# Where the weights' high and low parts are kept in a two-layer hybrid encoder, and in which order the first ones are made

## Chip, cores, metric

The kernel runs on one core of one Trainium2 chip. The metric is the device time of one execution in microseconds. The median of three runs of the kernel before is 1534.49 us (1534.33 to 1534.7).

## What is computed

Two layers over 256 tokens of width 1024, in float32. Each layer has a mixer (one wide projection, three kinds of attention, gates, output projections) and a mixture of experts, each behind an RMS norm whose scale and shift come from a conditioning vector:

```python
for l in range(DEPTH):                       # DEPTH = 2
    mod = c_act @ ada_w[l] + ada_b[l]
    shift_m, scale_m, gate_m, shift_f, scale_f, gate_f = split(mod, 6)
    h = rms_norm(x, mix_norm_g[l]) * (1 + scale_m) + shift_m
    z = h @ w_in[l]                          # 1024 x 7680: q, k, v of three mixers, 3 gates
    o_a, o_n, o_d = diff_attention(z), neighbourhood_attention(z), dilated_attention(z)
    merged = g_a * (o_a @ w_proj_a) + g_n * (o_n @ w_proj_n) + g_d * (o_d @ w_proj_d)
    x = x + gate_m * (merged @ w_out[l])
    h = rms_norm(x, ffn_norm_g[l]) * (1 + scale_f) + shift_f
    x = x + gate_f * hier_moe(h)             # 32 experts, top 2 of one of 4 groups
out = rms_norm(x, final_norm_g)
```

## The kernel before

**Products in two parts.** The projections (`z`, the three `w_proj`, `w_out`) are done with float32 operands cut in two: a high part that ACT makes by a copy to the type `float32r`, and a low part, the rest, that VectorE makes by a subtraction. A product is then three matmuls, high with high, high with low, low with high (`gemm`, L333). For the normalised input these parts are `hi` and `lo` (`modulated`, L277), for the weights `whi` and `wlo` (`split`, L322). `split` takes a piece of 128 x 1024 numbers: two slices of 128 rows of the contraction by 512 columns. Its two results lie in tiles with the tags `w4a` and `w4b`, each with two buffers, so two pieces can be held at a time; a buffer comes free when the matmuls that read it are done.

**Chunks.** `w_in` is worked through in 15 chunks of 512 columns (`chunk`, L442, with `SEGS`, L41): 0 to 8 are queries, keys and values, 9 to 14 the gates. A chunk loads its 2 MB of weights (`load`, L385, two half pairs, see below), takes some loads of the conditioning weights for later use (`FILL`, L200; `ada_part`, L155, each with products of 128x512 on VectorE at L175 and some on ACT at L173), and calls `gemm` over four pieces. One piece gives 24 matmuls of 256 columns, or the same in 512 columns. The results are moved out of PSUM when the next chunk reaches its third piece (`HOLD`, `flush`): a rotary segment (`place`, L476) costs four ACT copies (L484), two VectorE products (L485, L486) and one GpSimd addition (L487).

**The first pieces.** In chunk 0 the first two pieces are split ahead of `modulated` (L429), with `early=True`: the copies on ACT are kept in program order, and the subtraction runs on GpSimd. `modulated` then takes the reciprocal root of the mean square (`rsqrt`, ten small VectorE instructions), spreads it over the partitions by two matmuls, and for each of 8 slices scales (VectorE, L292), adds the shift (ACT, L294, giving `hi`), and takes the rest (VectorE, L289, giving `lo`). The last of the four transposed blocks of the input is copied from PSUM on VectorE (L272) just before.

**Memory.** `slots` holds ten pairs of 128 x 4096 numbers; `slot` (L77) hands out halves. In the mixer eleven halves are taken as long-lived tiles at its start (L396): three for the gates (`G`, of which the third also holds the rotary tables), two each for queries, keys and values, two for work (`T0`, `T1`); with the transposed input that is six pairs. The other four pairs carry the streams of `w_in` and of the conditioning weights. A one-element write by GpSimd (L398) makes each long tile taken early.

**Order.** The tile framework plans the order on each engine: among instructions that are ready in its own model of time, the one that is earlier in the program goes first, and a tile is given its place at its first write. `keep_in_program_order` pins one instruction behind the one traced before it on the same engine. On the chip every engine works its list in that order. The attention of a layer is spread among the chunks by the plan; so are the loads, all issued by SP.

**After the mixer** `moe` (L694) streams the experts' weights, 2 MB a load, through the same ten pairs.

Of the kernel before, what the change touches and what calls it, by code (L numbers as in the profile page):

```python
# [60 lines left out]
class Kernel:  # L61
# [197 lines left out]
    def raw_t(self, c):  # L259

        nc = self.nc
        p = self.acc()
        for kk in range(2):
            k = 2 * c + kk
            for t in range(2):
                nc.tensor.transpose(p[:, kk * 256 + t * P:kk * 256 + (t + 1) * P],
                                    self.x[:, t, k * P:(k + 1) * P], self.ident)
        to, p = self.xT[:, 2 * c:2 * c + 2, :], p.rearrange("p (k n) -> p k n", k=2)
        if c < 3:
            nc.scalar.copy(to, p)  # L270
        else:
            self.rest = lambda: self.tc.keep_in_program_order(nc.vector.tensor_copy(to, p))  # L272

    def hilo(self):
        return (self.wk.tile([P, KD, 256], F32R, name=nm, tag=tag) for nm, tag in (("hi", "w8a"), ("lo", "w8b")))

    def modulated(self, l):  # L277

# [9 lines left out]
        def low(k):  # L288
            nc.vector.scalar_tensor_tensor(lo[:, k, :], xT[:, k, :], shift[:, k:k + 1], hi[:, k, :].bitcast(F32),  # L289
                                           op0=OP.add, op1=OP.subtract)  # L290
        for k in range(KD):
            i = nc.vector.scalar_tensor_tensor(xT[:, k, :], xT[:, k, :], scale[:, k:k + 1], R,  # L292
                                               op0=OP.mult, op1=OP.mult)
            nc.scalar.activation(hi[:, k, :], xT[:, k, :], AF.Identity, bias=shift[:, k:k + 1])  # L294
            if k > 1:
                self.tc.keep_in_program_order(i)
            if k:
                low(k - 1)
        low(KD - 1)
        return hi, lo  # L300

# [19 lines left out]

    def split(self, w, early=False):  # L322

        nc, n = self.nc, w.shape[1]
        whi, wlo = (self.wk.tile([P, n, 1024 // n], F32R, name=f"{nm}{n}", tag=tag, bufs=2)
                    for nm, tag in (("whi", "w4a"), ("wlo", "w4b")))
        c = nc.scalar.copy(whi, w)  # L327
        if early:
            self.tc.keep_in_program_order(c)
        (nc.gpsimd if early else nc.vector).tensor_sub(wlo, w, whi.bitcast(F32))  # L330
        return whi, wlo
# [46 lines left out]
    def mixer(self, l, fill):  # L378
# [16 lines left out]
        M = self.xT.rearrange("p k n -> p (k n)")  # L395
        tiles = [self.slot("long") for _ in range(11)]  # L396
        for b in tiles:
            nc.gpsimd.memset(b[:, 2047:2048], 0.0)  # L398
        G, (Q0, Q1, K0, K1, V0, V1, T0, T1) = tiles[:3], tiles[3:]
        ga = [G[i // 4][:, 512 * (i % 4):512 * (i % 4 + 1)] for i in range(12)]  # L400
        tok = [M[:, t * D:(t + 1) * D] for t in range(2)]
# [6 lines left out]
        self.dmask = [K1[:, 1536:], V0[:, 1536:]]  # L408
        self.rope = G[2][:, 1536:].rearrange("p (c n) -> p c n", c=2)
        self.subg = T0[:, 1664:1792]  # L410
# [10 lines left out]
        if l == 0:  # L421
            self.new_sums()
            for t in range(2):
                for half in range(2):
                    hs = slice(half * 512, (half + 1) * 512)
                    self.square(t, half, self.x[:, t, hs], G[t][:, hs])
            for c in range(4):
                self.raw_t(c)
        halves = [self.split(w0[0][:, k:k + 2], True) for k in (0, 2)]  # L429
        hi, lo = self.modulated(l)  # L430

# [10 lines left out]
        def chunk(n):  # L442
# [28 lines left out]
            if n == 0:  # L471
                pieces[:2] = [(*p, h) for p, h in zip(pieces, halves)]
            self.gemm(pieces, hi, lo, prods)
# [20 lines left out]
        self.na_attention(l, qT, kT, vn, bias, oT[0])  # L494
        self.dil_attention(l, qT, kT, vd, oT[1])
        for n in range(9, 15):
            chunk(n)
# [631 lines left out]
```

## Time and profile before

| | |
|---|---|
| median of three runs | 1534.49 us |
| the profiled execution | 1535.39 us, span 1533.6 us |
| busy share of the span: TensorE, its weight loads | 80%, 52% |
| VectorE, ACT, GpSimd | 40%, 25%, 5% |
| DMA, mean rate | 355 GB/s, 543.93 MB in all |
| mean granted clock of TensorE | 0.911 of full |

Shares over the whole span hide that there are two kinds of stages. In the table of stretches each line begins with its bounds in us from the span's start; then come the busy time of each engine with its number of instructions, the granted share of TensorE's clock (1.0 is 2.4 GHz, 0.5 is 1.2 GHz), the share of the DMA engines and their rate. The view of waits says which instruction waited for which, how long in all, how often, and the longest. The timeline lists instructions by start and duration; in brackets stands the idle time before one, and what ended it. An instruction is named by engine, line, operation, and what it writes and reads.

### The profile page before, as it was taken

The page shows a single profiled execution, that of the slowest core. Times are in us where ns is not written, and L with a number is a line of the kernel's source. Part 1 is how long each engine was busy: PE and PEld are TensorE (multiplying, and loading weights), DVE is VectorE, ACT ScalarE, POOL GpSimd, SP SyncE. Part 2 cuts the span into 40 slices and gives each one's busy share as a digit, 9 for nine tenths or more (in the row PEclk, how much of TensorE's full clock was granted, in tenths as well). Part 3 has the DMA queues.
Part 4 walks back from the last instruction along what each step waited for, and adds up shares of the span by engine and source line. Part 5 has one row for each costly group of instructions (what it writes and reads, how often), then busy time and mean ns, then how long its engine had stood idle before and what let it go on. Part 6 is the DMA issues. An engine that isn't in the chain of part 4 may idle for free. (4 is left out here: it accounts for less than half of the span.)

```text
span 1533.6 us, 20114 instructions
## 1 busy us (share of the span) xinstructions
PE 1228.9 (80%) x8370; PEld 796.2 (52%) x8370; DVE 606.8 (40%) x1202; ACT 384.7 (25%) x681; POOL 73.4 (5%) x71
## 2 busy tenths in 40 slices
PE   5998999989777577677778899999897577577575
PEld 3888889874233133133257889899543133133132
DVE  2779884772112012011058797448322012011012
ACT  2656555450000000000046566544200000000001
POOL 1202000100000000000011110001000000000001
PEclk8999999999979889787889999999998788798898
DMA  9778683869999999999994874276899999999997
GB/s 369 284 296 319 275 326 146 343 246 403 428 425 427 427 427 427 427 426 428 421 372 172 340 312 186 110 315 235 318 425 426 427 426 427 427 426 427 426 427 294
DMA packets 52975, 543.93 MB, mean 355 GB/s; under 512 B 6784, under 2 KB 8336, under 8 KB 12048
## 3 DMA queue, kind: packets, MB, share of 16 engines
q1 hardware_dynamic: 52880, 542.60, 85.8%
q8 instruction: 68, 1.11, 0.3%
q14 instruction: 27, 0.22, 0.0%
HBM read 541.51 MB, written 1.06 MB: 354 GB/s over the span
## 5 line engine op out<-in xcount | busy, mean ns | idle before, releaser
L95 PE MATMUL acc<-rg,xg 128*32 128x512 f32 x2048 | 279.0, 687 | 116.3 <-DMA rg<-w 114.3
L95 PE MATMUL acc<-hi,wlo 128*128 128x256 f32 x896 | 260.0, 295 | 18.4 <-DVE wlo L330 18.0
L95 PE MATMUL acc<-lo,whi 128*128 128x256 f32 x896 | 253.4, 289 | 0.2 <-DVE lo L289 0.2
L95 PE MATMUL acc<-hi,whi 128*128 128x256 f32 x896 | 245.6, 290 | 6.5 <-ACT hi L294 4.9
L95 PE MATMUL acc<-rg,b 128*32 128x512 f32 (+1 forms) x1152 | 159.7, 688 | 93.7 <-DMA rg<-w2g 76.6
L95 PEld LDWEIGHTS acc<-rg,xg 128*32 128x32 f32 x2048 | 68.2, 118 | 303.7 <-issue 294.7
L330 DVE TENSOR_TENSOR wlo<-rg,whi 128x1024 fp32r<-128x1024 f32 x148 | 183.9, 1243 | 86.7 <-ACT whi L327 86.4
L327 ACT CAST whi<-rg 128x1024 fp32r<-128x1024 f32 x152 | 159.1, 1047 | 162.3 <-PE acc L95 136.1
L95 PEld LDWEIGHTS acc<-hi,wlo 128*128 128x128 f32 x896 | 175.1, 196 | 31.6 <-DVE wlo L330 24.2
L95 PEld LDWEIGHTS acc<-lo,whi 128*128 128x128 f32 x896 | 174.4, 196 | 1.6 <-DVE lo L289 0.5
L95 PEld LDWEIGHTS acc<-hi,whi 128*128 128x128 f32 x896 | 169.5, 196 | 10.5 <-ACT hi L294 5.5
L833 DVE TENSOR_TENSOR b<-b,acc 128x512 f32<-128x512 f32 x16 | 11.0, 687 | 350.5 <-PE acc L95 350.5
L95 PEld LDWEIGHTS acc<-rg,b 128*32 128x32 f32 x1152 | 35.5, 124 | 200.1 <-DMA rg<-w2g 112.6
L95 PEld LDWEIGHTS misc<-b,xn 128*128 128x128 f32 x512 | 124.6, 334 | 17.1 <-issue 15.7
L95 PE MATMUL misc<-b,xn 128*128 128x128 f32 x512 | 125.6, 404 | 4.1 <-DVEq L938 2.2
L832 ACT ACTIVATE b<-acc 128x512 f32<-128x512 f32 x16 | 9.6, 597 | 441.5 <-PE acc L95 441.5
L175 DVE SCALAR_TENSOR_TENSOR rg<-rg,sc 128x512 f32<-128x512 f32 x140 | 112.0, 832 | 4.4 <-DMA rg<-ada_w 2.5
L846 DVE TENSOR_TENSOR Y<-acc,grb 128x512 f32<-128x512 f32 x28 | 19.4, 692 | 235.5 <-PE acc L95 235.5
L826 ACT COPY b<-misc 128x256 f32<-128x256 f32 x16 | 6.0, 373 | 334.9 <-PE misc L825 334.9
L813 DVE TENSOR_SCALAR xg<-misc,mcol 128x128 f32<-128x128 f32 x128 | 44.3, 406 | 106.5 <-PE misc L95 106.5
L95 PE MATMUL acc<-wlo,hi 128*128 128x256 f32 (+1 forms) x256 | 79.8, 317 | 4.4 <-DVE wlo L330 4.3
L95 PE MATMUL acc<-whi,lo 128*128 128x256 f32 (+1 forms) x256 | 78.6, 314 | 1.5 <-DVE lo L310 1.3
(169 smaller groups left out, 1165.7 us busy)
## 6 DMA issues: line engine op xcount, KB each, us to landing
rg<-w SPq DMA_DIRECT2D x128, 2048.0 KB, 39.2
rg<-w2g SPq DMA_DIRECT2D x56, 2048.0 KB, 38.3
rg<-w_in SPq DMA_DIRECT2D x56, 1024.0 KB, 7.0
rg<-ada_w SPq DMA_DIRECT2D x48, 1024.0 KB, 8.5
rg<-w2c SPq DMA_DIRECT2D x12, 1024.0 KB, 29.6
rg<-w_proj SPq DMA_DIRECT2D x8, 1024.0 KB, 4.8
rg<-w_out SPq DMA_DIRECT2D x8, 1024.0 KB, 6.9
rg<-w_in SPq DMA_DIRECT2D x8, 512.0 KB, 15.4
```

The lines of the kernel that those rows point to most:

```text
L95: return self.nc.tensor.matmul(out, lhsT, rhs, start=start, stop=stop, **kw)
L175: V.scalar_tensor_tensor(to, to, self.sc[:, k:k + 1], w[:, 0, cs] if j else self.ada_sum[:, cs], op0=OP.mult, op1=OP.add)
L327: c = nc.scalar.copy(whi, w)
L330: (nc.gpsimd if early else nc.vector).tensor_sub(wlo, w, whi.bitcast(F32))
L813: nc.vector.tensor_scalar(xg[:, k, :], p[:, kk * P:(kk + 1) * P], gf[:, k:k + 1], sf[:, k:k + 1], op0=OP.mult, op1=OP.add)
L826: nc.scalar.copy(ST, p[:, :256])
L832: nc.scalar.activation(a, h1, AF.Silu)
L833: nc.vector.tensor_mul(a, a, h3)
L846: nc.vector.tensor_mul(Y[:, hs], y[half], self.grb[:, hs])
```

## The change

`split` no longer has `early`. It takes its place from a rotating list `homes`: for chunks 0 to 8 that is two halves of a new pair (`parts`), each with a high and a low part in it, and then twice the old tiles, so four pieces can be held. From the gates' chunks on the list is `[None]`, the old two buffers. The subtraction is always on VectorE. All four pieces of chunk 0 are split inside `modulated`, ahead of slices 0, 2, 4 and 6; there the copy, the subtraction and every scaling are pinned in program order. The copy of the last transposed block goes from VectorE to ACT. At the mixer's start nine long tiles are taken in place of eleven; the gates' first two are taken after the attention, ahead of chunk 9, with their own one-element writes. The squares of layer 0 write their scratch to `T0` and `T1`.

```diff
--- before.py
+++ after.py
@@ -269,12 +269,13 @@
         if c < 3:
             nc.scalar.copy(to, p)
         else:
-            self.rest = lambda: self.tc.keep_in_program_order(nc.vector.tensor_copy(to, p))
+            self.rest = lambda: self.tc.keep_in_program_order(nc.scalar.copy(to, p))
 
     def hilo(self):
         return (self.wk.tile([P, KD, 256], F32R, name=nm, tag=tag) for nm, tag in (("hi", "w8a"), ("lo", "w8b")))
 
-    def modulated(self, l):
+    def modulated(self, l, w):
+
 
         nc, xT = self.nc, self.xT
         hi, lo = self.hilo()
@@ -288,16 +289,18 @@
         def low(k):
             nc.vector.scalar_tensor_tensor(lo[:, k, :], xT[:, k, :], shift[:, k:k + 1], hi[:, k, :].bitcast(F32),
                                            op0=OP.add, op1=OP.subtract)
+        parts = []
         for k in range(KD):
+            if k % 2 == 0:
+                parts.append(self.split(w[k // 2], self.tc.keep_in_program_order))
             i = nc.vector.scalar_tensor_tensor(xT[:, k, :], xT[:, k, :], scale[:, k:k + 1], R,
                                                op0=OP.mult, op1=OP.mult)
             nc.scalar.activation(hi[:, k, :], xT[:, k, :], AF.Identity, bias=shift[:, k:k + 1])
-            if k > 1:
-                self.tc.keep_in_program_order(i)
+            self.tc.keep_in_program_order(i)
             if k:
                 low(k - 1)
         low(KD - 1)
-        return hi, lo
+        return hi, lo, parts
 
     def to_hilo(self, src, done):
 
@@ -319,15 +322,18 @@
             two(k, p.rearrange("p (a n) -> p a n", a=2))
         return hi, lo
 
-    def split(self, w, early=False):
+    def split(self, w, keep=lambda i: None):
 
         nc, n = self.nc, w.shape[1]
-        whi, wlo = (self.wk.tile([P, n, 1024 // n], F32R, name=f"{nm}{n}", tag=tag, bufs=2)
-                    for nm, tag in (("whi", "w4a"), ("wlo", "w4b")))
-        c = nc.scalar.copy(whi, w)
-        if early:
-            self.tc.keep_in_program_order(c)
-        (nc.gpsimd if early else nc.vector).tensor_sub(wlo, w, whi.bitcast(F32))
+        to = self.homes.pop(0)
+        self.homes.append(to)
+        if to is None:
+            whi, wlo = (self.wk.tile([P, n, 1024 // n], F32R, name=f"{nm}{n}", tag=tag, bufs=2)
+                        for nm, tag in (("whi", "w4a"), ("wlo", "w4b")))
+        else:
+            whi, wlo = (to[:, i:i + 1024].rearrange("p (k n) -> p k n", k=n).bitcast(F32R) for i in (0, 1024))
+        keep(nc.scalar.copy(whi, w))
+        keep(nc.vector.tensor_sub(wlo, w, whi.bitcast(F32)))
         return whi, wlo
 
     def gemm(self, pieces, hi, lo, prods):
@@ -393,11 +399,15 @@
             return w
         w0 = load(0)
         M = self.xT.rearrange("p k n -> p (k n)")
-        tiles = [self.slot("long") for _ in range(11)]
-        for b in tiles:
-            nc.gpsimd.memset(b[:, 2047:2048], 0.0)
-        G, (Q0, Q1, K0, K1, V0, V1, T0, T1) = tiles[:3], tiles[3:]
-        ga = [G[i // 4][:, 512 * (i % 4):512 * (i % 4 + 1)] for i in range(12)]
+
+        def take(n, of):
+            tiles = [self.slot(of) for _ in range(n)]
+            for b in tiles:
+                nc.gpsimd.memset(b[:, 2047:2048], 0.0)
+            return tiles
+        G2, Q0, Q1, K0, K1, V0, V1, T0, T1 = take(9, "long")
+        self.homes = [self.slot("parts"), self.slot("parts"), None, None]
+        ga = []
         tok = [M[:, t * D:(t + 1) * D] for t in range(2)]
         qT2, kT2 = ([X[i // 4][:, 512 * (i % 4):512 * (i % 4 + 1)] for i in range(6)] for X in ((Q0, Q1), (K0, K1)))
         qT, kT = ([a.rearrange("p (a n) -> p a n", a=2) for a in X] for X in (qT2, kT2))
@@ -406,7 +416,7 @@
         vd = V0[:, :1536].rearrange("p (t n) -> p t n", t=2)
         bias = V1.rearrange("p (t h n) -> p t h n", t=2, h=4)
         self.dmask = [K1[:, 1536:], V0[:, 1536:]]
-        self.rope = G[2][:, 1536:].rearrange("p (c n) -> p c n", c=2)
+        self.rope = G2[:, 1536:].rearrange("p (c n) -> p c n", c=2)
         self.subg = T0[:, 1664:1792]
         vdst = {"va": va, "vn": vn, "vd": vd}
         turn = {}
@@ -423,11 +433,10 @@
             for t in range(2):
                 for half in range(2):
                     hs = slice(half * 512, (half + 1) * 512)
-                    self.square(t, half, self.x[:, t, hs], G[t][:, hs])
+                    self.square(t, half, self.x[:, t, hs], (T0, T1)[t][:, hs])
             for c in range(4):
                 self.raw_t(c)
-        halves = [self.split(w0[0][:, k:k + 2], True) for k in (0, 2)]
-        hi, lo = self.modulated(l)
+        hi, lo, halves = self.modulated(l, [w0[k // 4][:, k % 4:k % 4 + 2] for k in range(0, KD, 2)])
 
         def late_loads():
             if l == 0:
@@ -469,7 +478,7 @@
                     evac.append(lambda z=z, kind=kind, dst=dst: place(z, kind, (qT2 if kind[1] == "q" else kT2)[dst]))
             pieces = [(k, w[k // 4][:, k % 4:k % 4 + 2]) for k in range(0, KD, 2)]
             if n == 0:
-                pieces[:2] = [(*p, h) for p, h in zip(pieces, halves)]
+                pieces = [(*p, h) for p, h in zip(pieces, halves)]
             self.gemm(pieces, hi, lo, prods)
             self.pending += evac
 
@@ -493,6 +502,9 @@
         oT = [tok[i][:, 512:].rearrange("p (a n) -> p a n", a=2) for i in range(2)]
         self.na_attention(l, qT, kT, vn, bias, oT[0])
         self.dil_attention(l, qT, kT, vd, oT[1])
+        self.homes = [None]
+        G = take(2, "gates") + [G2]
+        ga += [G[i // 4][:, 512 * (i % 4):512 * (i % 4 + 1)] for i in range(12)]
         for n in range(9, 15):
             chunk(n)
         self.flush()
```

## Rows read from the trace of the kernel before

**Rows 1.** Stretches, bounds in us; columns as explained above.

```profile
48.00:84.00 36.00, 31.75 (x204) 26.96 (x203) 30.44 (x43) 23.75 (x39) 8.59 (x4) 1.00 0.69 275
84.00:108.00 24.00, 24.00 (x200) 23.45 (x199) 14.21 (x18) 13.30 (x17) 0.00 (x0) 1.00 0.79 302
108.00:146.00 38.00, 32.90 (x241) 30.55 (x239) 37.07 (x46) 21.38 (x31) 10.86 (x5) 0.91 0.72 288
...
200.00:266.00 66.00, 65.37 (x501) 57.98 (x500) 43.40 (x104) 34.14 (x67) 0.00 (x0) 1.00 0.56 215
...
350.00:770.00 420.00, 309.64 (x1883) 128.23 (x1883) 62.96 (x138) 14.49 (x32) 0.76 (x11) 0.86 1.01 426
...
794.00:842.00 48.00, 42.87 (x294) 37.20 (x293) 38.47 (x50) 30.12 (x45) 8.04 (x4) 1.00 0.49 199
...
854.00:916.00 62.00, 55.93 (x403) 50.52 (x402) 57.47 (x80) 36.85 (x60) 12.98 (x6) 0.97 0.82 326
```

**Rows 2.** TensorE's waits in 31:84, 108:146, 794:842, 854:916; total, times, longest.

```profile
PE acc L95 <- DVE wlo L330: 4.2, 5, 1.3
...
PE acc L95 <- DVE wlo L330: 5.0, 3, 3.5
...
PE acc L95 <- DVE wlo L330: 5.1, 8, 1.5
...
PE acc L95 <- DVE wlo L330: 5.9, 4, 3.4
```

**Rows 3.** Stretches behind the two longest waits of rows 2.

```profile
137.80:143.10 5.30, 5.30 (x25) 5.30 (x26) 5.30 (x7) 0.20 (x1) 2.79 (x1) 0.50 0.72 298
877.20:880.40 3.20, 3.20 (x15) 3.20 (x16) 3.20 (x4) 0.00 (x0) 1.93 (x1) 0.50 0.25 102
```

**Rows 4.** ACT's waits in 31:167, the first layer's chunks.

```profile
ACT whi L327 <- PE acc L95: 34.1, 17, 5.8
```

**Rows 5.** Timeline of ACT and GpSimd in chunk 1 of layer 0.

```profile
48.81 2.34 ACT L484 COPY rg<-acc 32x512 f32<-32x512 f32 x4 [1.11 <-PE acc L95]
51.18 1.05 ACT L327 CAST whi<-rg 128x1024 fp32r<-128x1024 f32 x1
52.26 2.34 ACT L484 COPY rg<-acc 32x512 f32<-32x512 f32 x4
...
52.62 2.13 POOL L487 TENSOR_TENSOR rg<-rg 128x512 f32<-128x512 f32 x1 [16.86 <-DVE rg L486]
```

**Rows 6.** Timeline of VectorE ahead of the longest wait of rows 2.

```profile
134.20 2.42 DVE L175 SCALAR_TENSOR_TENSOR rg<-rg,sc 128x512 f32<-128x512 f32 x2
136.54 1.21 DVE L330 TENSOR_TENSOR wlo<-rg,whi 128x1024 fp32r<-128x1024 f32 x1
```

**Rows 7.** Timeline of GpSimd and VectorE at the head of layer 1's mixer.

```profile
779.59 4.64 POOL L330 TENSOR_TENSOR wlo<-rg,whi 128x1024 fp32r<-128x1024 f32 x2 [0.66 <-ACT whi L327]
...
779.60 2.35 DVE L239 SCALAR_TENSOR_TENSOR rsq<-rsq 128x2 f32<-128x2 f32 x1
781.98 2.26 DVE L240 TENSOR_TENSOR rsq<-rsq 128x2 f32<-128x2 f32 x1
...
784.77 0.69 DVE L272 COPY rg<-acc 128x512 f32<-128x512 f32 x1
786.01 0.87 DVE L292 SCALAR_TENSOR_TENSOR rg<-rg,mcol,acc 128x256 f32<-128x256 f32 x2 [0.54 <-PE acc L95]
```

**Rows 8.** Timeline of VectorE at the head of layer 0's mixer.

```profile
30.95 0.17 DVE L195 TENSOR_TENSOR mcol<-adap,acol 128x8 f32<-128x8 f32 x1 [0.67 <-PE adap L193]
31.15 2.31 DVE L214 SCALAR_TENSOR_TENSOR mcol<-mcol,gcol 128x8 f32<-128x8 f32 x1
```

**Rows 9.** The page's group of the subtractions (mean 1243 ns), and one shift on ACT.

```profile
L330 DVE TENSOR_TENSOR wlo<-rg,whi 128x1024 fp32r<-128x1024 f32 x148 | 183.9, 1243 | 86.7 <-ACT whi L327 86.4
...
790.34 0.51 ACT L294 ACTIVATE hi<-rg,mcol 128x256 fp32r<-128x256 f32 x1 [0.22 <-DVE rg L292]
```

**Rows 10.** Stretch of the first three pieces of chunk 0 in layer 1.

```profile
787.10:798.00 10.90, 10.90 (x74) 10.90 (x75) 8.02 (x16) 5.38 (x9) 0.00 (x0) 0.79 0.85 350
```

## The prediction, made before the changed kernel was run

> **What bounds the kernel now.** I read the busy table by stretch first, because a share over the whole span would mix two regimes [rows 1]. From 350 to 770 us the DMA engines are full (share 1.01) and the rest waits for expert weights; nothing of the change lies there. The other part of each layer, the mixer, is different: between 200 and 266 us the DMA share is 0.56 while TensorE has work for 65.37 of 66 us. So a mixer that ends earlier lets the DMA-bound stage begin earlier by as much, and a microsecond taken out of TensorE's row in the mixer should come off the span.
>
> Then I asked what TensorE waits for in the chunks for queries, keys and values. In four stretches the answer is the same group: the low part `wlo`, which VectorE writes at L330. It is 4.2 us in 5 waits (31:84), 5.0 in 3 (108:146), 5.1 in 8 (794:842) and 5.9 in 4 (854:916), together 20.2 us in 20 waits [rows 2]. Behind two of them the granted clock stands at 0.50, the 1.2 GHz level, for 5.30 and 3.20 us of work [rows 3]; at the level 1.00, which most of these stretches show, the same work takes half, so these tails cost 2.65 and 1.6 us. In all 24.45 us.
>
> Why is `wlo` late? The cast that makes `whi` on ACT waits for TensorE 34.1 us in 17 waits in the first layer's chunks [rows 4]. There are two places for `whi`, so the cast of piece n needs the matmuls of piece n-2 to be done. When a place comes free, ACT has often just begun a rotary evacuation: the four copies of L484 take 2.34 us from 48.81, and the cast follows at 51.18 [rows 5]. The other form of the wait is VectorE's own queue: at 134.20 it begins two products of the modulation weights, 2.42 us, and the difference that TensorE needs starts only at 136.54 [rows 6].
>
> At the head of a mixer another row stands out. In layer 1 GpSimd makes the first two low parts from 779.59 for 4.64 us. Beside that, two VectorE instructions of the reciprocal root, on two numbers per partition, take 2.35 and 2.26 us [rows 7]; one of that kind takes 0.17 without GpSimd beside it, as L195 in layer 0 [rows 8]. They lie on the chain to the first scaled input at 786.01, and TensorE has nothing else. In layer 0 the same befalls L214: 2.31 us [rows 8].
>
> **The change, part by part.** All sums are against the profiled execution, 1535.39 us (span 1533.6); the median of the runs shown is 1534.49, 0.9 us less.
>
> *GpSimd out of the first pieces, layer 1.* Removed from the chain: 2.35 + 2.26 - 2 x 0.17 = 4.27 us. Added: a difference of 1.24 us on VectorE [rows 9] ahead of the first scaling. It fits a hole: L240 ends at 784.24, two instructions of 0.17 end the root, and the scaling starts at 786.01, some 1.4 us later, in which TensorE spreads the root and VectorE did the copy L272, 0.69 us [rows 7]. That copy goes to ACT, which waits there. So the first scaling comes at about 786.0 - 4.3 = 781.7, and the first matmul, which began 1.1 us after it [rows 10], at 782.8. The fixed order then makes VectorE wait for each cast. A round is two scalings (0.87), an activation and the cast on ACT (0.51 and 1.05), and the difference (1.24): 3.7 us [rows 5, 7, 9]. The last piece can start after three rounds, one scaling and one activation, 781.7 + 11.0 + 1.0 = 793.7. TensorE took 10.90 us for three pieces, a part of it at 1.2 GHz [rows 10], so it gets there at 793.7 too: just fed. Gain 4.0 us, between 1.5 (rounds a microsecond longer) and 4.3.
>
> *The same in layer 0.* L214 gives back 2.31 - 0.17 = 2.1 us, but the difference (1.24) now stands ahead of the first scaling with nothing beside it, since this chain waits for the modulation column and not for the root. Net 0.9 at the first scaling; then the rounds, with the lambda parameters' small steps between. I take +0.5 us, between -1 and +1.3. A pair must be free for the new places by then: eleven long tiles and the input made six of the ten pairs, now nine and the input make five and the places one, so the count is the same.
>
> *Four places instead of two.* A cast now waits for piece n-4, two pieces sooner: 48 matmuls at 24.00 us for 200 of them (84:108 in [rows 1]) are 5.8 us. All waits of [rows 2] are shorter (3.5 at most), so ACT is no longer the limit. VectorE may be: a wait comes back only if VectorE has time to do its work sooner. So I weigh by its busy time [rows 1].
> - 48:84: VectorE 30.44 of 36 us, 5.6 idle for 4.2 of waits. I take two thirds, 2.8; bounds 1.5 to 4.2.
> - 108:146: VectorE 37.07 of 38, full. Waits and slow clock 5.0 + 2.65 = 7.65 us. Two more pieces done ahead are 2.5 us, and the weights' slots come free two pieces sooner, so that the modulation weights, for want of which VectorE had only 14.21 of 24 us in 84:108, land sooner. I take half, 3.8; bounds 0 to 7.65.
> - 794:842: VectorE 38.47 of 48, 9.5 idle for 5.1: two thirds, 3.4; bounds 1 to 5.1.
> - 854:916: VectorE 57.47 of 62; 5.9 + 1.6 = 7.5, half, 3.75; bounds 0 to 7.5.
>
> Sum 13.75 us, bounds 2.5 to 24.45. After these stretches TensorE is full again (200:266) and VectorE is not (43.40 of 66), so what is won isn't waited away there.
>
> *The gates' two tiles.* They are no longer held from the start but taken after the attention, by one-element writes that wait for nothing but a free pair. These may take one before the places are given back, so a load of chunk 9 or of the modulation comes one release later. Attention work stands between. Cost 0; bound 2 us a layer.
>
> *No cost.* The squares' scratch in T0 and T1 is free before the attention; fewer one-element writes at the head are off every path.
>
> Sum: 4.0 + 0.5 + 13.75 = 18.25 us. 1535.39 - 18.25 = 1517.1 for an execution like the profiled one, 1516.2 against the median.
>
> **A rule that speaks against it.** The Trainium skill, "Perfetto Trace Analysis", section "Identifying the Most-Contended Engine", says to improve the engine with the highest occupancy first. In 108:146 and 854:916 that engine is VectorE [rows 1], to which the change gives work (two differences for one copy in each layer). By the rule these stretches would give nothing; this is the second rival below.
>
> **The rivals.**
> 1. *All waits come back.* ACT and VectorE work far enough ahead, since VectorE is idle for 9.8 us in 84:108 and full only later. 24.45 + 4.5 = 29 us: 1505.5. Against it: VectorE stays full in 108:146, and the modulation's products come earlier in the program than the differences, so the planner places them first when both are ready.
> 2. *VectorE is the bound.* The places fill up, but VectorE's queue does the same work in the same order, and TensorE waits later for what it doesn't wait for now. Then the head of layer 1 counts and a little of the rest: 4.5 to 7.5 us, 1527 to 1530; if the rounds eat the head too, 1532 to 1534. For it: 37.07 of 38 us. Against it: thirteen of the twenty waits lie in stretches with VectorE idle for longer than they last.
> 3. *Slower: the two new places count as one.* Both are halves of one pair. If a write to one half had to wait for the readers of the other, each chunk would have a cast and a difference in the open, 1.05 + 1.24 = 2.3 us, at 8 chunks in 2 layers 36.6 us, in place of 24.45 us of waits and less 4.5 us at the heads: 7.7 us more, 1542.2. It decides from 29 / 16 = 1.8 us of open work a chunk. Against it: ACT writes the next place in T1 from 52.26, while GpSimd reads another place of the same tile from 52.62 for 2.13 us [rows 5]; parts of one tile don't wait for each other there.
>
> **How the numbers follow.** Forecast 0.46, rival 1 0.16, rival 2 0.25, rival 3 (with any other loss by a worse order) 0.13. 0.2% is 3.1 us, about what a measurement of this kernel can tell from no change. Faster: 0.46 + 0.16 + 0.15 of rival 2 = 0.77; within 0.2%: the other 0.10 of rival 2; slower 0.13. The forecast alone spans 1509 to 1525. The range for 8 in 10 reaches from 1503, where all waits and both heads at their best (24.45 + 5.6 = 30 us) would nearly lead, to 1532; it leaves out rival 3 and the worst of rival 2.
>
> **What would show it.** Right: no VectorE instruction of 2 us in layer 1's root, and its first matmul of chunk 0 about 4 us sooner after the last square; casts that wait for TensorE far less than 34 us a layer; waits for `wlo` near 10 us instead of 20.2; no stretch at 1.2 GHz in the middle of the chunks. Wrong: the same 20 us of waits under another name (`acc`, `hi`), a `wlo` that follows its cast at once and is late all the same, or TensorE waiting at the end of the attention for what was won before it.

## The result, and the profile after

The changed kernel takes 1509.38 us (median; 1508.2 to 1510.29) beside 1534.6 us of the kernel before: ratio 0.9835, 95% interval 0.9818 to 0.9852. That is 25.2 us less, where 18.25 were forecast. The profiled execution took 1509.41 us, its span 1507.6.

The reduction that ends each sum of squares (L256, VectorE) marks the start of mixer 0, its end, the start of mixer 1, its end, and the end. In the timeline of the changed kernel (start, duration, instruction):

```profile
14.78 0.16 DVE L256 TENSOR_REDUCE rstd<-ssq 128x2 f32<-128x6 f32 x1 [2.28 <-ACT rg L251]
325.75 0.16 DVE L256 TENSOR_REDUCE rstd<-ssq 128x2 f32<-128x10 f32 x1 [0.92 <-ACT acc L251]
768.98 0.16 DVE L256 TENSOR_REDUCE rstd<-ssq 128x2 f32<-128x10 f32 x1 [0.64 <-ACT misc L251]
1055.51 0.16 DVE L256 TENSOR_REDUCE rstd<-ssq 128x2 f32<-128x10 f32 x1 [0.92 <-ACT acc L251]
```

The same rows of the kernel before stand at 14.98, 335.07, 778.61 and 1082.00. So mixer 0 ends 9.3 us sooner and mixer 1 is 16.9 us shorter (286.53 for 303.39); the first layer's experts take 443.2 us in the changed kernel and 443.5 before, as they should when only their start moves. The two layers must be read apart.

Waits of TensorE for the parts of the weights (what waited, total, times, longest), to be held against [rows 2]. The first three rows are from 31:260, the last from 770:1000:

```profile
PE acc L95 <- DVE wlo L336: 2.4, 3, 1.6
...
PE acc L95 <- ACT rg L335: 1.1, 2, 0.6
...
PE acc L95 <- DVE rg L336: 0.8, 1, 0.8
...
PE acc L95 <- DVE wlo L336: 4.1, 5, 1.7
```

The parts in the new places bear the name `rg`, those in the old ones `whi` and `wlo`. So the waits for the low part (L336) are 3.2 and 4.1 us, where the kernel before had 11.2 in 31:260 and 11.1 in 778:1010: about two thirds of them are gone. ACT's casts wait for TensorE in 31:167 by the next two rows, 17.3 us in 10 waits instead of 34.1 in 17 [rows 4]:

```profile
ACT whi L335 <- PE acc L95: 12.1, 6, 3.3
...
ACT rg L335 <- PE acc L95: 5.2, 4, 1.8
```

The stretches of layer 0 (columns as in [rows 1]; the last two were chosen at the attention's end, and behind them stands 255:275 of the kernel before):

```profile
48.00:84.00 36.00, 35.43 (x236) 30.66 (x236) 31.69 (x44) 23.69 (x39) 7.26 (x4) 1.00 0.83 329
84.00:108.00 24.00, 24.00 (x203) 24.00 (x202) 17.34 (x21) 14.18 (x18) 2.14 (x1) 1.00 0.69 271
108.00:146.00 38.00, 36.44 (x269) 33.64 (x268) 38.00 (x46) 24.52 (x36) 9.72 (x7) 1.00 0.71 276
160.00:220.00 60.00, 58.64 (x455) 51.87 (x456) 52.72 (x129) 33.40 (x69) 0.00 (x0) 1.00 0.80 314
220.00:255.00 35.00, 34.30 (x264) 30.78 (x264) 18.11 (x43) 20.23 (x38) 0.00 (x0) 1.00 0.46 181
255.00:275.00 20.00, 17.10 (x119) 14.03 (x120) 7.68 (x20) 8.46 (x19) 0.00 (x0) 0.83 0.56 222
264.90:271.70 6.80, 6.21 (x32) 4.92 (x33) 1.71 (x3) 2.73 (x6) 0.00 (x0) 0.50 0.97 410
...
255.00:275.00 20.00, 19.21 (x154) 17.61 (x152) 10.55 (x22) 11.46 (x20) 0.00 (x0) 1.00 0.29 107
```

Three things are to be seen. TensorE has work for 35.43 of 36 us where it had 31.75. In 108:146 VectorE is full to the last (38.00 of 38), and TensorE still runs for 36.44 where it had 32.90, at full clock; one wait of 1.6 us for the low part is left there. So a full VectorE holds it far less than before. And there is a new weak place, 255:275, with TensorE at 17.10 of 20 and, in its second half, at 1.2 GHz (0.50); the kernel before had 19.21 of 20 there at 1.00.

Mixer 1 as a whole, before and then changed:

```profile
778.61:1082.00 303.39, 281.05 (x2104) 257.60 (x2104) 219.22 (x376) 166.19 (x283) 32.77 (x17) 0.97 0.63 249
...
768.98:1055.51 286.53, 275.03 (x2104) 253.37 (x2104) 216.03 (x378) 165.37 (x284) 26.23 (x17) 0.99 0.67 265
```

For the same 2104 matmuls TensorE is idle for 11.5 us instead of 22.3, and busy for 6.0 us less, with a granted clock of 0.99 instead of 0.97.

The head of layer 1, VectorE and TensorE:

```profile
769.97 0.16 DVE L239 SCALAR_TENSOR_TENSOR rsq<-rsq 128x2 f32<-128x2 f32 x1
770.17 0.16 DVE L240 TENSOR_TENSOR rsq<-rsq 128x2 f32<-128x2 f32 x1
...
770.93 1.22 DVE L336 TENSOR_TENSOR rg<-rg 128x1024 fp32r<-128x1024 f32 x1 [0.21 <-DMA rg<-subg]
772.07 0.86 DVE L296 SCALAR_TENSOR_TENSOR rg<-rg,mcol,acc 128x256 f32<-128x256 f32 x2
...
773.14 0.95 PE L95 MATMUL acc<-hi,rg 128*128 128x256 f32 x4 [1.59 <-ACT hi L298]
```

The first matmul comes 4.16 us after the reduction, where it came 8.48 after (787.09 - 778.61): 4.3 us.

### The profile page after: what moved, and what is told of

It reads as the page before. It is cut to its first block, busy times and chain, and to the rows that moved or that the text cites. A ratio compares the mean times of both kernels' runs of the same rounds, so it can differ in the third digit from the quotient of the medians.

```text
span 1507.6 us, 20134 instructions
## 1 busy us (share of the span) xinstructions
PE 1224.9 (81%) x8370; PEld 789.9 (52%) x8370; DVE 601.9 (40%) x1204; ACT 383.2 (25%) x683; POOL 59.5 (4%) x67
## 5 line engine op out<-in xcount | busy, mean ns | idle before, releaser
L95 PE MATMUL acc<-rg,xg 128*32 128x512 f32 x2048 | 280.1, 689 | 115.1 <-DMA rg<-w 113.1
L95 PE MATMUL acc<-hi,wlo 128*128 128x256 f32 x704 | 199.9, 288 | 5.7 <-DVE wlo L336 5.5
L95 PE MATMUL acc<-lo,whi 128*128 128x256 f32 x704 | 196.7, 285 | 0.0
L95 PE MATMUL acc<-hi,whi 128*128 128x256 f32 x704 | 192.6, 287 | 0.1
L336 DVE TENSOR_TENSOR wlo<-rg,whi 128x1024 fp32r<-128x1024 f32 x116 | 147.0, 1268 | 62.6 <-ACT whi L335 58.7
L335 ACT CAST whi<-rg 128x1024 fp32r<-128x1024 f32 x116 | 121.5, 1048 | 90.8 <-PE acc L95 82.7
L95 PEld LDWEIGHTS acc<-hi,wlo 128*128 128x128 f32 x704 | 134.9, 192 | 12.3 <-DVE wlo L336 7.7
L95 PEld LDWEIGHTS acc<-lo,whi 128*128 128x128 f32 x704 | 134.1, 191 | 2.8 <-issue 2.2
L95 PEld LDWEIGHTS misc<-b,xn 128*128 128x128 f32 x512 | 124.7, 334 | 18.3 <-issue 16.9
L95 PEld LDWEIGHTS acc<-hi,whi 128*128 128x128 f32 x704 | 131.1, 192 | 2.9 <-issue 1.7
L95 PE MATMUL acc<-hi,rg 128*128 128x256 f32 x384 | 74.6, 292 | 4.9 <-ACT hi L298 3.4
L95 PE MATMUL misc<-Y,b 128*128 128x512 f32 (+1 forms) x144 | 63.8, 582 | 4.9 <-DVE Y L798 4.9
```

The costliest lines, as they stand in the source:

```text
L95: return self.nc.tensor.matmul(out, lhsT, rhs, start=start, stop=stop, **kw)
L335: keep(nc.scalar.copy(whi, w))
L336: keep(nc.vector.tensor_sub(wlo, w, whi.bitcast(F32)))
```

## The experiments

All runs in one table. A ratio is against the kernel before on the same chip (its medians there: 1533.3 to 1534.9). "Attention 0" is where ACT's last copy of layer 0's attention starts (the fourth row of L703 in the timeline, other lines elsewhere), "mixer 0" the mark at its end, "mixer 1" the length between its two marks.

| kernel | us | ratio, 95% | attention 0 | mixer 0 | mixer 1 |
|---|---|---|---|---|---|
| before | 1534.6 | | 280.1 | 335.07 | 303.4 |
| changed | 1509.38 | 0.9835 (0.9818 to 0.9852) | 270.2 | 325.75 | 286.5 |
| e1 places only | 1514.72 | 0.9881 (0.9866 to 0.9896) | 269.4 | 324.36 | 293.2 |
| e2 heads only | 1529.97 | 0.9974 (0.9965 to 0.9983) | 279.1 | 334.55 | 297.8 |
| e5 GpSimd back | 1507.40 | 0.9830 (0.9817 to 0.9843) | 269.5 | 324.43 | 286.0 |
| e8 fewer products beside | 1552.81 | 1.0121 (1.0105 to 1.0136) | 296.1 | 351.08 | 306.6 |
| e9 three places | 1517.31 | 0.9880 (0.9864 to 0.9897) | 278.3 | 333.86 | 288.9 |
| e3 modulation late | 1516.50 | 0.9893 (0.9878 to 0.9908) | 276.7 | 331.64 | 288.8 |
| e11 modulation early | 1516.79 | 0.9884 (0.9868 to 0.9901) | 277.7 | 332.52 | 287.3 |
| e7 blocks in acc | 1513.29 | 0.9876 (0.9861 to 0.9891) | 276.9 | 328.73 | 285.9 |
| e13 attention sooner | 1521.74 | 0.9907 (0.9893 to 0.9920) | 277.0 | 332.83 | 291.5 |
| e10 without products | (1503.77) | work left out | 264.1 | 319.06 | 286.8 |

### The two parts alone: e1 and e2

e1 undoes the head, e2 the places (both shortened):

```diff
 # e1: the changed kernel with four places, but
-        hi, lo, halves = self.modulated(l, [...])
+        halves = [self.split(w0[0][:, k:k + 2], True) for k in (0, 2)]   # differences on GpSimd
+        hi, lo = self.modulated(l)
 # e2: the kernel before with two places, but in modulated
+            if k % 2 == 0 and k < 4:
+                parts.append(self.split(w[k // 2], self.tc.keep_in_program_order))
```

> The four places, without the new head: the first two pieces are split early with their differences on GpSimd, the last block is copied by VectorE, as before. Theory (the places give back the chunks' waits in both layers, the heads give 4.3 and 1.3 us by themselves): 25.2 - 5.6 = 19.6 us less than before, about 1515 us, range 1513 to 1517; the head of layer 1 still takes 8.5 us from the sum of squares to the first matmul. Rival (the fixed order of the first four pieces is what puts VectorE ahead of TensorE, and the places alone give what I forecast, 13.75 us or less): 1521 to 1527, with waits for the low part left in 31:84 and 794:842.

> The new head alone, with the two old places: the first two differences on VectorE in a fixed order ahead of slices 0 and 2, the copy of the last block on ACT; pieces 3 and 4 are split by the plan. Theory (the two parts add up): 4.3 us in layer 1, up to 1.3 in layer 0, 1529 to 1531 us. Rival (with two places the third piece waits for the first one's matmuls, so that a head which starts sooner runs into that wait): 0 to 2.5 us less than before, 1532 to 1534.5.

Both theories held. e1 saves 1.19% (18.3 us), e2 0.26% (4.0 us), together 22 of 25. By marks: layer 1 gives 10.2 us for the places and 5.6 for the head, 15.8 of 16.9; in e1 the waits for the low part fall to 2.6 and 1.1 us in the two layers. Layer 0 gives 10.7 for the places and 0.5 for the head, though its first matmul comes 1.2 us sooner in e2 (33.47 for 34.66). There the parts don't add up: the places alone end mixer 0 at 324.36, 1.4 us before the whole change does.

### GpSimd back: e5

Shortened; GpSimd's subtraction isn't pinned:

```diff
         keep(nc.scalar.copy(whi, w))
-        keep(nc.vector.tensor_sub(wlo, w, whi.bitcast(F32)))
+        nc.gpsimd.tensor_sub(wlo, w, whi.bitcast(F32))      # the first two pieces
```

> The changed kernel with the first two differences of chunk 0 back on GpSimd; order, places and the copy on ACT stay. Theory (a difference on GpSimd beside the reciprocal root holds two of its small VectorE instructions for 2.3 us each, and that is the head's gain of layer 1): two instructions over 2 us in layer 1's root again, its first matmul of chunk 0 about 8.4 us after the sum of squares instead of 4.16; in layer 0 one held instruction, but its microseconds are lost at the end of the attention anyway. 1512.5 to 1515. Rival (the gain of the head comes from the order and from the copy on ACT, and GpSimd's work overlaps the root without harm): 1508.5 to 1510.5.

The theory fell. Timeline of e5, VectorE and GpSimd (its sum of squares is reduced at 767.79):

```profile
769.36 0.16 DVE L242 SCALAR_TENSOR_TENSOR rsq<-rsq 128x2 f32<-128x2 f32 x1
770.39 0.87 DVE L296 SCALAR_TENSOR_TENSOR rg<-rg,mcol,acc 128x256 f32<-128x256 f32 x2 [0.87 <-DMA rg<-dmask]
...
773.20 2.30 DVE L290 SCALAR_TENSOR_TENSOR lo<-rg,mcol,hi 128x256 fp32r<-128x256 f32 x1
...
769.40 2.35 POOL L337 TENSOR_TENSOR rg<-rg 128x1024 fp32r<-128x1024 f32 x1 [1.29 <-ACT rg L335]
772.83 2.39 POOL L337 TENSOR_TENSOR rg<-rg 128x1024 fp32r<-128x1024 f32 x1 [1.09 <-ACT rg L335]
```

GpSimd does the same work and nothing is lost: its first difference begins at 769.40, when the root is done (L242 at 769.36), because ACT makes the cast before it only behind the copy of the last block. In e1, with the old order and the copy on VectorE, the cast comes at 768.17, GpSimd begins at 769.28 in the middle of the root, and two steps there take 2.21 and 2.26 us. ACT in e5, then GpSimd and VectorE in e1:

```profile
767.79 0.59 ACT L272 COPY rg<-acc 128x512 f32<-128x512 f32 x1
768.27 1.05 ACT L335 CAST rg<-rg 128x1024 fp32r<-128x1024 f32 x1
...
769.28 4.69 POOL L336 TENSOR_TENSOR rg<-rg 128x1024 fp32r<-128x1024 f32 x2 [0.66 <-DMA rg<-dmask]
...
769.48 2.21 DVE L240 TENSOR_TENSOR rsq<-rsq 128x2 f32<-128x2 f32 x1
771.73 2.26 DVE L241 TENSOR_TENSOR rsq<-rsq 128x2 f32<-128x2 f32 x1
```

So the head's gain is one of order, not of the engine. The fixed order and the copy on ACT were not tried one without the other; together they put GpSimd's start behind the root. The hold itself is real: L290 takes 2.30 us beside GpSimd here, 0.47 without.

### Is a full VectorE the cause of the waits? e8

```diff
 # the kernel before
-    FILL = (0, 1, 0, 3, 0, 2, 2, 3, 2, 2, 3, 2, 3, 0, 1), (0, 0, 2, 2, 2, 2, 2, 2, 1, 3, 0, 0, 0, 0, 0)
+    FILL = (0, 1, 0, 3, 0, 1, 1, 1, 3, 3, 4, 3, 3, 0, 1), (0, 0, 2, 2, 1, 1, 0, 0, 1, 3, 2, 2, 2, 0, 0)
```

> The kernel before with its two places, with modulation loads and their VectorE products taken out of the chunks in which VectorE was full: in layer 0 four loads of chunks 5 to 7 go to chunks 8 to 11, in layer 1 six of chunks 4 to 7 go to chunks 10 to 12. Theory (two places set the waits: a cast needs the matmuls of piece n-2, and then VectorE is late with the difference whether it is full or not): waits for the low part of 4 us or more stay in the stretch 108:146, and the time is within 3 us of before, 1531 to 1537. Rival (the forecast's step: a full VectorE makes about half of these waits): 3 to 4 us of them go in each layer, 1526 to 1531.

Stretch 108:146 of e8, and TensorE's waits in it:

```profile
108.00:146.00 38.00, 30.99 (x215) 27.79 (x214) 25.82 (x31) 19.91 (x28) 10.37 (x5) 0.91 0.57 222
...
PE acc L95 <- DVE wlo L330: 5.0, 2, 4.2
```

VectorE goes from 37.07 busy us to 25.82, and the waits for the low part stay at 5.0 us. In layer 1 (870:932 for 854:916) VectorE goes from 57.47 to 45.23, and 4.7 us in 4 waits are left of 5.9. So the rival's 3 to 4 us a layer don't go: with two places there are waits of this size without a full VectorE. They aren't the same waits, though. ACT, VectorE and TensorE at the longest one of e8:

```profile
118.11 2.35 ACT L484 COPY rg<-acc 32x512 f32<-32x512 f32 x4
120.48 1.05 ACT L327 CAST whi<-rg 128x1024 fp32r<-128x1024 f32 x1
...
121.54 1.21 DVE L330 TENSOR_TENSOR wlo<-rg,whi 128x1024 fp32r<-128x1024 f32 x1
...
122.81 0.58 PE L95 MATMUL acc<-hi,wlo 128*128 128x256 f32 x1 [4.17 <-DVE wlo L330]
```

Here ACT casts late, behind a rotary evacuation, and the difference follows at once. In the kernel before, the cast for the longest wait begins at 132.65 and lasts 1.05 us, and the difference comes 2.8 us behind its end, at 136.54 [rows 6]: that wait was VectorE's queue. With two places either route makes a wait; that two more places take most of both away is shown by e1, not by e8. The time was missed: 19.5 us slower, since the products that were moved now stand beside layer 0's attention, which ends at 296.1 instead of 280.1.

### How many places: e9

```diff
-        self.homes = [self.slot("parts"), self.slot("parts"), None, None]
+        self.homes = [self.slot("parts"), None, None, self.slot("parts")][:3]
-            if k % 2 == 0:
+            if k % 2 == 0 and k < 6:
```

> The changed kernel with three places in turn instead of four; at the head three pieces are split in the fixed order, the fourth by the plan. Theory (every wait before but three was shorter than the 2.9 us of one piece's 24 matmuls, so one more place gives nearly all): within 4 us of the changed kernel, 1509 to 1513. Rival (each place gives its share, so that half of the 19 us which the places give is lost): 1517 to 1521.

By its time the rival won, by layers each has one half: mixer 1 takes 288.9 us, 2.4 more than with four places and 8.9 less than with two (e2), as the theory had it. Mixer 0 ends at 333.86, 0.7 sooner than with two. Its chunks run ahead (the cast of the last gates chunk's first piece is at 238.4, between 229.1 with four places and 247.9 before), but its attention ends at 278.3. (Of two further kernels with three places the times, 1589.8 and 1584.36 us, aren't used: there the fourth piece of chunk 0 overwrote the first before its products, so that the experts had other tokens; those of layer 0 took 503 and 495 us.)

### What holds the end of layer 0: e10, e3, e11, e7, e13

In 255:275 of the changed kernel TensorE has no chunk left; it waits for small steps of the dilated attention, as at 265.49:

```profile
264.65 0.16 DVE L694 RECIPROCAL dl_s<-dl_s 128x1 f32<-128x1 f32 x1 [0.94 <-ACT rg L693]
264.85 0.49 DVE L695 TENSOR_SCALAR rg<-rg,dl_s 128x512 f32<-128x512 f32 x1
...
265.49 0.44 PE L592 MATMUL misc<-k,rg 128*128 128x128 f32 x1 [1.60 <-DVE rg L695]
...
270.17 0.27 ACT L703 COPY rg<-misc 128x128 f32<-128x128 f32 x1 [1.31 <-PE misc L95]
```

e10 leaves 28 of VectorE's products out:

```diff
+                    if l == 1 and s < 2 and (j or h % self.CHAIN):
+                        continue
```

> The changed kernel, but 28 of VectorE's products and 2 of ACT's kind stay: the products of the eight loads for layer 1's first two modulation columns are left out, all but the first of each column, so that layer 1 computes with other columns; only the end of mixer 0 is read (325.75 us in the changed kernel by its sum of squares). Theory (VectorE's products beside the attention hold its chain in layer 0; some 25 us of them stand in chunks 10 to 14): mixer 0 ends 5 us or more sooner, below 321. Rival (the chain of small steps from engine to engine is as long without them): 324 to 327. In between would mean that both have a part.

Mixer 0 ends at 319.06, 6.7 us sooner: the theory's side. Its stretches, and the only wait of TensorE in 160:260:

```profile
160.00:220.00 60.00, 59.52 (x454) 51.87 (x454) 39.02 (x116) 35.07 (x78) 0.00 (x0) 1.00 0.78 313
220.00:255.00 35.00, 35.00 (x286) 32.40 (x286) 17.27 (x35) 18.64 (x34) 0.00 (x0) 1.00 0.37 138
255.00:275.00 20.00, 18.89 (x163) 17.80 (x159) 11.85 (x17) 10.65 (x17) 1.55 (x2) 1.00 1.01 424
...
PE misc L95 <- ACT rg L596: 0.5, 1, 0.5
```

VectorE has 39.02 busy us in 160:220 instead of 52.72, the attention ends at 264.1 instead of 270.2, and TensorE stays at full clock. So VectorE's products beside the attention do hold it. (ACT's products of these columns stay, four in the trace.) How much of the 6.1 us is VectorE's own and how much TensorE's clock, which doesn't fall here, wasn't separated. Four kernels tried to use this without leaving work out, and all were slower than the changed one:

```diff
 # e3, e11: layer 0's loads per chunk, changed kernel: 0, 1, 0, 3, 0, 2, 2, 3, 2, 2, 3, 2, 3, 0, 1
+    FILL = (0, 1, 0, 3, 0, 2, 2, 3, 2, 1, 1, 1, 2, 2, 4), ...    # e3
+    FILL = (0, 1, 1, 3, 2, 2, 3, 3, 2, 2, 2, 2, 1, 0, 0), ...    # e11
 # e7, to_hilo
-            p = self.misc()
+            p = self.acc()
 # e13, mixer: diff_attention inside the loop over chunks
+            if n == 6:
+                self.diff_attention(l, qT, kT, va, tok)
-        self.diff_attention(l, qT, kT, va, tok)
```

> The changed kernel with seven of layer 0's loads of the modulation weights, with their products on VectorE, taken in chunks 13 and 14 instead of 9 to 11 (2, 1, 1, 1, 2, 2, 4 loads in chunks 8 to 14 in place of 2, 2, 3, 2, 3, 0, 1). Theory (in layer 0 the attention's chain sets the end of the mixer now, and VectorE, busy for 52.7 of 60 us in 160:220 with these products too, holds that chain): mixer 0 ends 4 to 8 us sooner, 1501 to 1505 us. Rival 1 (the chain's steps follow each other through five engines' queues, and VectorE's load has no part in it): 1508 to 1510. Rival 2 (the products that are moved now stand behind the attention and ahead of the output projection): slower, 1511 to 1515.

> The changed kernel with three to four of layer 0's loads of the modulation weights taken earlier: 0, 1, 1, 3, 2, 2, 3, 3, 2, 2, 2, 2, 1, 0, 0 loads in chunks 0 to 14 in place of 0, 1, 0, 3, 0, 2, 2, 3, 2, 2, 3, 2, 3, 0, 1, so that their products fall where VectorE was idle for 6.7 of 24 us (84:108) and not beside the attention. Theory (products beside the attention lengthen it): mixer 0 ends 2 to 6 us sooner, 1503 to 1507. Rival 1 (the chunks need VectorE as it is: waits for the low part come back): 1511 to 1516. Rival 2 (the attention's length is its own): 1508 to 1510.

> The changed kernel with the transposed blocks ahead of the output projections in the four accumulators (acc) instead of the three misc buffers, for which they compete with the attention. Theory (at the end of layer 0 TensorE has no work but the attention's short steps, because the first output projection, whose input is long done, waits for a misc buffer until 267; it also falls to 1.2 GHz there): with other buffers its products fill these holes; mixer 0 ends 4 to 8 us sooner, layer 1 up to 3: 1499 to 1505. Rival (the last block of the attention ends when it ends, and the second output projection waits for it however much was done before): 1507 to 1510. Rival 2 (the blocks hold accumulators which the gates' chunks need): slower, 1511 to 1516.

> The changed kernel with the first of the three attentions, which needs chunks 0 to 2 alone, put ahead of chunks 7 and 8 in the program; no work is added or taken away. Theory (in layer 0 the end of the mixer is set by an attention that begins at 146 and is stretched by VectorE's products; VectorE is idle for 6.7 of 24 us in 84:108 and TensorE has slack at the attention's end): an attention that begins sooner ends sooner, mixer 0 by 3 to 7 us, layer 1 within 2: 1502 to 1507. Rival 1 (its steps take VectorE and ACT from the chunks 5 to 8, in which VectorE is full, so that TensorE waits there for what it doesn't wait for at the end): 1509 to 1516. Rival 2 (the plan has begun the attention as soon as its work tiles, which the rotary steps share, come free, and the order of the program changes little): 1508 to 1510.5.

In e3 VectorE's work in 220:255 rose from 18.11 to 24.98 us, with 13 of the products, where the dilated attention runs. The time is that of rival 2 (1.5 us above its range), but not its place: the products stand beside the attention and not behind it. In e11 the weights of the chunks come later; ACT's casts in 84:160 (idle time before them and what ended it), e11 and then the changed kernel:

```profile
L335 ACT CAST rg<-rg 128x1024 fp32r<-128x1024 f32 x8 | 8.0, 1050 | 7.4 <-DMA rg<-w_in 7.4
```

```profile
L335 ACT CAST rg<-rg 128x1024 fp32r<-128x1024 f32 x8 | 8.3, 1048 | 5.5 <-PE acc L95 4.1 <-DMA rg<-w_in 1.3
```

7.4 us for want of `w_in` instead of 1.3. The time is that of rival 1 (0.8 us above its range), but TensorE's waits for the low part did not come back (2.2 us in 31:260); the transfers are what the trace shows instead. In e7 the output projection does fill the hole, so that mixer 0 ends 51.8 us after the attention; but the attention's last steps now stand behind it, and it ends at 276.9. The time lies in rival 2's range, not by its reason. In e13 the second head of the attention begins at 128 instead of 151, and still the last one ends at 277.0, with TensorE at 54.69 of 60 us in 160:220 and mixer 1 5.0 us longer; its time lies above all three ranges.

The table has the rule in it. Mixer 0's mark less the attention's last copy, from unrounded times: 55.0 (before), 55.6 (changed), 55.0 (e1), 55.4 (e2), 54.9 (e5), 54.9 (e8), 55.5 (e9), 54.9 (e3), 54.9 (e11), 54.9 (e10), 55.8 (e13); e7, which moves work out of this stretch, has 51.8. In layer 0 the mixer's end hangs on the end of the attention, before the change too. In layer 1 the same difference was 61.4 us before (1082.00 - 1020.63) and is 54.9 now (1055.51 - 1000.65). What came last there is seen in ACT's last copy of the attention (L691, now L703) and its last evacuation of a gate (L467, now L476), before and then changed:

```profile
1020.63 0.27 ACT L691 COPY rg<-misc 128x128 f32<-128x128 f32 x1
...
1024.50 0.59 ACT L467 ACTIVATE rg<-acc 128x512 f32<-128x512 f32 x1
...
996.51 0.59 ACT L476 ACTIVATE rg<-acc 128x512 f32<-128x512 f32 x1
...
1000.65 0.27 ACT L703 COPY rg<-misc 128x128 f32<-128x128 f32 x1 [0.43 <-PE misc L95]
```

Before, the gates' chunks ended after the attention, so TensorE's own backlog came last; now the attention does. In layer 0 the attention came last already before the change (280.1 against 271.7 for the gate).

## Why the prediction was right, and where its sizes were off

The time lies in the range, 7 us under the forecast. That alone says little: the range holds every gain from 2.5 to 31.5 us, and the time is nearer to rival 1 (1505.5) than to the forecast (1516.2), at the edge of the forecast's own span (1509 to 1525). What speaks for the mechanism is the split by e1 and e2 and the waits that went. Term by term:

- **Head of layer 1**, 4.0 forecast: 4.3 at the first matmul, 5.6 at the mixer's end (e2). The size was right, the reason half: what was named as taking GpSimd out is the order (e5). That TensorE would be "just fed" by the rounds was right: TensorE waits for nothing in the 17 us behind its first matmul.
- **Head of layer 0**, 0.5 forecast: 1.2 to 1.3 us at the first matmul, 0.5 at the mixer's end (e2), where the attention decides.
- **Four places**, 13.75 forecast: 20.9 by marks in e1 (10.7 and 10.2). This is the term that was mis-sized, by the step "a wait comes back only if VectorE has time to do its work sooner": the halves and two thirds taken by VectorE's busy share. In 108:146, with VectorE full, the waits fell from 5.0 to 1.6 us and the slow clock behind them is gone, 6.05 us of 7.65 where half was taken. The stretches of layer 1, moved by its earlier start, have 1.0 us left of 5.1 (784.4:832.4) and 2.7 of 5.9 (844.4:906.4, without the slow clock of 1.6): 4.1 and 4.8 us where 3.4 and 3.75 were taken. Only 31:84 gave less, 2.3 us for 2.8 (1.9 of 4.2 are left, 1.1 of them for the high part). That is 17.25 us; it isn't traced where the rest of the 20.9 comes from. The slow tails were put a little too high: by [rows 1, 3] their 40 matmuls took 0.21 us each beside 0.12 at full clock, which makes 2.3 and 1.4 us, not 2.65 and 1.6.
- **Rival 1** (all waits come back) is near in layer 1, but not the case: 4.1 of 11.1 us of waits are left. Mixer 1's 16.9 us are 10.8 of idle time, mostly waits for the low part (7.0 less) and for the root (4.3 less), and 6.0 of matmuls that run faster. The clock gave more than the one tail that was counted.
- **"What is won isn't waited away"** after the chunks: wrong for layer 0. There the last gate is evacuated at 252.87 instead of 271.66, 18.8 us sooner, and 9.3 arrived; in layer 1 it is 18.4 sooner (counted from the mixer's start), and 16.9 arrived. The argument looked at VectorE's mean share in 200:266 [rows 1]; what counts is a chain, the attention, and it moved by 9.9 us (280.1 to 270.2). The prediction had named this as a sign that it would be wrong. So the two errors are of opposite sign: too little for the places, too much for what reaches the end. That they partly cancel is luck.
- **Rival 2** (VectorE as the bound) fell by 108:146 and e8, and with it the rule of the Trainium skill, "Perfetto Trace Analysis", section "Identifying the Most-Contended Engine", for these stretches: the engine with the highest occupancy was not the one to relieve. e10 is a stretch where relieving VectorE does pay, 160:220, and there it was fuller before than any other engine but TensorE as well; occupancy alone doesn't tell the two apart.
- **Rival 3** (the halves of one pair count as one) fell: no wait of 2.3 us in each chunk, and casts that wait half as long.
- **The gates' tiles**, 0 forecast. They stand behind the attention only in the program: on the chip the one-element writes (L406) run at 133.62 and 871.36, long before the attention ends. Behind them ACT's casts wait 0.3 us for `w_in` in layer 0 and not at all in layer 1. The bound of 2 us held.

What stays open: why three places give nearly all in layer 1 and almost nothing in layer 0. In layer 0 the attention ends at 278.3 there, and TensorE's granted clock in 255:280 is 0.73 beside 0.86 with four places (e3 has 0.73 too, e11 0.93); which of the attention's steps the plan put later, and what the clock makes of it, wasn't tried. Nor was a version found that beats the changed kernel: e5's interval overlaps its own.

## What to carry to other kernels

If an operand buffer is waited for through a chain (matmul, cast, difference), look at when the first step could start, not at how full the last engine is: a full queue gives way when its work may come in another order, and more places allow that. Before a gain is booked, ask in each stage which chain its end hangs on, and check it by a difference that stays constant over variants, such as the 55 us here, and by which of the two last results is the later one. And when an engine delays its neighbour, try a later start of the same work before moving it to another engine.

## What the runs showed of the hardware

Beside a GpSimd subtraction of two inputs, a VectorE instruction with two inputs in SBUF that begins after it lasts until just after GpSimd is done, with two numbers a partition as with 256: 2.21 us for L240 in e1, 2.30 for L290 at 773.20 in e5, and 0.58 for L290 at 771.45, where GpSimd had 0.3 us left. L296, with one input in PSUM, takes 0.87 for two beside it (770.39 in e5) and 0.86 without (772.07 in the changed kernel). The Trainium skill, "SBUF — State Buffer", section "Who interferes with whom", says that a VectorE instruction with two SBUF inputs contends with a GpSimd instruction that reads SBUF; the trace agrees.

The rotary additions on GpSimd do the same in the middle of the chunks, which the forecast's sum has no term for. GpSimd in the kernel before, and GpSimd and VectorE at the one wait that is left in 108:146 of the changed kernel:

```profile
134.43 1.64 POOL L487 TENSOR_TENSOR rg<-rg 128x512 f32<-128x512 f32 x1 [8.88 <-DVE rg L486]
...
130.76 1.67 POOL L496 TENSOR_TENSOR rg<-rg 128x512 f32<-128x512 f32 x1 [1.89 <-ACT rg L335]
...
131.20 2.30 DVE L336 TENSOR_TENSOR wlo<-rg,whi 128x1024 fp32r<-128x1024 f32 x1
```

The two products of 134.20 took 2.42 us beside the first of these [rows 6], and 1.40 without GpSimd (133.43 in the changed kernel); the subtraction of 131.20 took 2.30 instead of 1.21. So about 1 us of the longest wait before, and of the one that is left, is GpSimd's.

The clock went to 1.2 GHz at 264.9 after TensorE had been busy for 7.59 of 9.9 us in 255:264.9, on small matmuls with gaps. Four matmuls of L592 take 0.63 us at 263.25, and 1.08 for the next four, at 265.49. In e10 the 15 us ahead of the attention's end (249.1:264.1) have TensorE busy for 13.89 us and show 1.00 throughout. So a chain that leaves TensorE waiting cost twice here, once in gaps and once in the clock behind them.
